# A hybrid attention and HGRN layer: gates in pieces, meta rows in 34 columns, and casts and splits pinned in order

## The chip, the cores and the metric

The kernel runs on one core of a Trainium2 chip. The core has five engines with queues of their own: TensorE (PE) multiplies matrices, VectorE (DVE), ScalarE (ACT) and GpSimd (POOL) work on tiles, and SyncE (SP) issues transfers. An engine takes the instructions of its queue in order, and one that waits holds up all behind it. The metric is device time in microseconds (us), the median of several runs.

## The reference

The kernel computes one decoder layer in float32. 16 meta tokens are put ahead of 1024 tokens, which makes 1040 rows of 1024 columns. Cut to what matters:

```python
a = rmsnorm(h, ln_mix_pre)
dq, dk, dv, hq, hf, hi, hg = split(a @ w_in)            # 1024 -> 7 x 512
y_diff = diff_attention(dq, dk, dv, ...)                # 4 heads, blocks of 128 rows, 2 maps each
y_hgrn = hgrn2(hq, hf, hi, hg, lb, gnorm)               # 4 heads, chunks of 16 rows
h = h + rmsnorm(concat(y_diff, y_hgrn) @ w_out, ln_mix_post)
u = conv1d(rmsnorm(h, ln_ffn_pre) @ w_up)               # 1024 -> 5632, 3 taps per channel
gate, up = split(u)
h = h + rmsnorm((gelu(gate) * up) @ w_down, ln_ffn_post)
return h[:, 16:]                                        # without the meta rows
```

## The kernel before

Every large product is made of three matmuls. An operand `x` is split into a high part, which ACT casts to the format that TensorE reads, and a low part, which POOL or DVE gets by subtracting the high part from `x`; the products high·high, high·low and low·high are added up in PSUM. For weights these are `wh` (high) and `wl` (low), made from the raw tile `wr` that a DMA has brought. `load_split` does this for one tile of 128 x 512, and `load_m` for the two tiles of a projection. The normalised input of the layer is kept in the same way, as `ahi` and `alo`, 8 slices of 128 rows by 1040 tokens.

The program runs in stages.

- *Heads.* For each of four heads the three projections of the attention (`dq`, `dk`, `dv`) and the four of the HGRN part (`hf`, `hq`, `hi`, `hg`) are made, in this order. Each goes over three groups of tokens (16+256, 384 and 384), 24 matmuls to a group, into a PSUM tile `pi_<name>_<group>`; `ev_q`, `ev_k`, `ev_v` and others take it out to SBUF (for `hg`: three ACT operations and one of DVE that make a sigmoid, `sg`). While PE makes the projections of the attention part, the HGRN part of the head before runs between the matmuls (tiles `pl`, `pd`, `mix`, `po`); while it makes those of the HGRN part, the attention blocks do (`S` scores, `pt` transposes, `at`, `pa` the weighted sum). `dense` is the generator of the projections; it takes the weights of the first projection itself and loads one projection ahead; `flush` sends out work that has been put off. `interleave` mixes the generators by the costs that they yield, and so sets PE's order.
- *Differences of the down weights.* `down_sums` loads four tiles of `w_down` at a time, subtracts them in pairs on DVE and stores the results, in pieces between the groups of projections.
- *Output projection.* `out_part` makes the product of the mixed rows with `w_out`, 8 slices k, in two halves of 512 columns. Block 0, the 16 meta rows, has only two rows that are worked out here; `out_meta` makes them with `out_part`: three matmuls for each k, with two columns of `m0` as the stationary side.
- *Up projection.* Tiles `ft` of channels, each with a gate side (`ug`) and an up side (`uu`), and each in two halves of the tokens, p=0 and 1. Sums of weights and of inputs replace one of the eight products (7 products in a `unit`, in PSUM tiles `pa`, `pb`, `pc`; partial results `x`, `u`). A unit ends with the convolution: ACT makes the first tap (`conv`'s activation), DVE adds the two others (`SCALAR_TENSOR_TENSOR` on a tile `c`), ACT applies gelu, POOL multiplies the two sides. `prep` makes the splits of the weights for the next `ft`.
- *Down projection*, in the same way, and the end of the layer.

What sets the order: on PE the instructions stand as the program writes them. On the other queues a scheduler of the framework orders them, by data and its own estimate, unless `issue_after` (`tc.issue_after(x)`, and `behind(...)` built on it) puts an instruction behind another one in its queue.

Of the kernel before, what the change touches and what calls it, by code (L numbers as in the profile page):

```python
# [17 lines left out]
P = 128  # L18
# [4 lines left out]
KD = D // P  # L23
# [22 lines left out]
class Ordered:  # L46
# [3 lines left out]
    def __getattr__(self, name):  # L50
        call = getattr(self.engine, name)

        def issue(*args, **kw):
            ins = call(*args, **kw)  # L54
            return self.tc.keep_in_program_order(ins) if self.state["ordered"] else ins

        return issue
# [29 lines left out]
def layer_kernel(ctx: ExitStack, tc: tile.TileContext, x, meta, table, lbl, gpre, gpost, win,  # L87
# [65 lines left out]

    def split(hi, lo, raw, eng=None):
        A.copy(hi, raw)
        (eng or G).tensor_tensor(lo, raw, hi.bitcast(F32), op=ALU.subtract)
# [23 lines left out]
    at_cm, atp = pool("at", 1)  # L180
    ahi = atp.tile([P, KD, L], F32R, tag="ahi", name="ahi")
    alo = atp.tile([P, KD, L], F32R, tag="alo", name="alo")
    ws_cm, wsp = pool("wdsums", 5)

    last_load = []
# [42 lines left out]
    def proj_step(pt, parts, k, t0, t1, evac):  # L228
        cost = max(115.0, 0.42 * (t1 - t0))
        hi, lo = parts[k // 4]  # L230
        s = slice(P * (k % 4), P * (k % 4 + 1))
        T.matmul(pt, hi[:, s], ahi[:, k, t0:t1], start=(k == 0), stop=False)
        yield cost
        T.matmul(pt, hi[:, s], alo[:, k, t0:t1], start=False, stop=False)
        yield cost
        T.matmul(pt, lo[:, s], ahi[:, k, t0:t1], start=False, stop=(k == KD - 1))
        if k == KD - 1:
            evac()
        yield cost
# [35 lines left out]
    def pre_hi(pv, ks, s):  # L275
        return A.copy(ahi[:, ks, s], pv)

    def pre_lo(pv, ks, s):
        return V.tensor_tensor(alo[:, ks, s], pv, ahi[:, ks, s].bitcast(F32), op=ALU.subtract)

# [303 lines left out]
    def attn_in(h):  # L584
# [8 lines left out]
        def ev_q(g, b0, b1, t0, t1, pt):  # L593
            for m in range(2):
                A.mul(qs[m][own[m], t0:t1], pt[own[m]], 0.125)
                V.scalar_tensor_tensor(qs[m][oth[m], t0:t1], pt[own[m]], 0.125, qs[m][own[m], t0:t1].bitcast(F32), ALU.mult, ALU.subtract)

        def ev_k(g, b0, b1, t0, t1, pt):
            for m in range(2):
                A.copy(ks[m][own[m], t0:t1], pt[own[m]])  # L600
                V.tensor_tensor(kl[m][own[m], t0:t1], pt[own[m]], ks[m][own[m], t0:t1].bitcast(F32), op=ALU.subtract)
                A.copy(ks[m][oth[m], t0:t1], pt[own[m]])

# [7 lines left out]
    def attn(h, tens):  # L611
# [128 lines left out]

    def dense(tiles, preload=None, side=iter(())):
        parts = preload
        for idx, (m, name, evac) in enumerate(tiles):
            if parts is None:
                parts = load_m(m, name)
            nxt = load_m(tiles[idx + 1][0], tiles[idx + 1][1]) if idx + 1 < len(tiles) else None
            for g in range(3):
                next(side, None)
                for step, c in enumerate(proj_group(g, parts, name, evac)):
                    if step == 8:  # L750
                        flush()
                    yield c
            parts = nxt
# [173 lines left out]

    def load_wo(n, k):
        raw = wp.tile([P, 512], F32, tag="wr", name=f"wor{n}_{k}", bufs=3)
# [7 lines left out]
        hi, lo = (where.tile([P, 512], F32R, tag=t, name=f"{t}{n}_{k}", bufs=bufs) for t in tag)  # L937
        split(hi, lo, raw, V if n or k else G)
        return hi, lo
# [4 lines left out]
    def mix_split(i, k0, k1):  # L944
        r, t0 = tok(i)
        src = mix(slice(k0, k1), t0, t0 + r)
        if i < 2:
            m = (m0, kept)[i]
            hi, lo = m[:, 0, k0:k1], m[:, 1, k0:k1]
        elif k1 - k0 == 1:  # L950
# [25 lines left out]

    def out_meta(py, wo, nk):
        return out_part((m0[:, 0], m0[:, 1], 0, nk, 2), py, wo, True, True)

# [33 lines left out]
    def out_first():  # L1013
# [5 lines left out]
        for j in range(2):  # L1019
# [3 lines left out]
            A.copy(y0[:, FIRST[j]], pys[j])  # L1023
        for n, i in enumerate(FIRST[2:]):
            for k in ((0, 1), (2, 3), (4,), (5,), (6,), (7,))[n]:
                wo.append(load_wo(1, k))
            if n == 3:
# [6 lines left out]
            yield from out_part(sq_, py, wo0, False, True)  # L1034
            A.copy(y0[:, i], py)
        py = ps_in("py0_0")
        yield from out_meta(py, wo0, 7)
        A.copy(y0[:2, 0], py[:2])
        while 0 not in finished:
# [176 lines left out]
    for n, i in enumerate(order):  # L1216
# [5 lines left out]
        if i < 2:  # L1222
            m = (m0, kept)[i]
            todo = [(m[:, 0, a:a + 2], m[:, 1, a:a + 2], a, a + 2, tok(i)[0]) for a in range(0, KD, 2)]
        else:
            todo = ms + [pre_last[i]]
        nxt = []
        for c, part in enumerate(todo):
# [8 lines left out]
            if c == 3 and n >= 2:  # L1237
                trans(order[n - 2])
            for _ in out_part(part, py, wo, c == 0, part is todo[-1]):
                pass  # L1240
# [13 lines left out]
        if i == 3:  # L1254
            prep_plain(1, ("12", "22"))
        post_a(i, py)
    post_b(8)
# [19 lines left out]

    def conv(ft, p, side, u):
# [4 lines left out]
        V.scalar_tensor_tensor(c, u[:, 1:1 + w], cwt[:, m, 1:2], c, ALU.mult, ALU.add)  # L1283
        V.scalar_tensor_tensor(c, u[:, 0:w], cwt[:, m, 0:1], c, ALU.mult, ALU.add)
        return c

    def gated(ft, p, ug, uu, cu=None):
        cg = conv(ft, p, 0, ug)
        A.activation(cg, cg, AF.Gelu_apprx_tanh)
        cu = cu or conv(ft, p, 1, uu)  # L1290
        G.tensor_tensor(cg, cg, cu, op=ALU.mult)  # L1291
        st = SY.dma_start(gsc[P * ft: P * (ft + 1), 2 * HALF * p:2 * HALF * (p + 1)], cg)
        if ft < 2 and p == 0:
            marks["store"] = st

    waiting = []

    def plain_unit(ft, p, bank):
# [17 lines left out]
        if ft and p:  # L1316
            waiting.extend(us)
        else:
# [4 lines left out]
    def unit(ft, p, bank):  # L1323
# [39 lines left out]
        seam(p, (ug, uu))  # L1363
        gated(ft, p, ug, uu)
        yield
# [56 lines left out]
    for ft in range(2, NF):  # L1422
        units = [unit(ft, p, ps_b) for p in range(2)]
        for j in range(7):
            if j > 3 or ft > 2:
                prep(7 * (ft + 1) + j)
            for p, u in enumerate(units):
                next(u)
                if (ft, j, p) == (2, 3, 0):
                    with behind("u3", "x1"):  # L1430
                        cu = conv(1, 1, 1, waiting[1])
            if (ft, j) == (2, 3):
                with behind("u3", "shift"):
                    for q in range(4):
                        prep(21 + q)
                    gated(1, 1, *waiting, cu)
        if ft == NF - 3:
# [285 lines left out]
```

## Time and profile before

| | |
|---|---|
| time, median of 3 runs | 1327.34 us (1326.83 to 1329.81) |
| profiled execution | 1325.77 us, its span 1324.0 us |
| TensorE busy | 1276.6 us, 96%, 10227 matmuls |
| VectorE busy | 912.8 us, 69% |
| ScalarE busy | 689.4 us, 52% |
| GpSimd busy | 413.5 us, 31% |
| mean granted clock of TensorE | 0.994 |

The span is the time from the first to the last instruction in one profiled execution. A busy share is an average over all stages. In the profile a row of the timeline gives the start in us, the duration in us, the engine, the line of the kernel, the operation, the tile written and the tiles read, and the shape; in brackets stands how long the engine was idle ahead of it and what released it. Buffer numbers are left out there (`wh_dq` is any tile of that name). Where a helper records the operation all rows have its line, L54. A row of grouped instructions gives least, median and most ns.

### The profile page before, as it was taken

How to read it: one execution, taken by the hardware profiler on the slowest of the kernel's cores; microseconds unless marked ns; L12 is line 12 of the kernel's file. 1: busy time of each engine (PE TensorE's matmuls, PEld its weight loads, DVE VectorE, ACT ScalarE, POOL GpSimd, SP SyncE). 2: the span in 40 equal slices, each digit the busy share in tenths (PEclk: the TensorE clock that was granted, in tenths of full speed). 3: DMA queues.
4: the chain of work that ended last, by engine and by line, in shares of the span. 5: the costliest groups of instructions: out<-in, count | busy, mean ns of one | idle time of the engine just before them, and what ended most of it. 6: DMA issues, size and time to landing. Idle time of an engine off the chain costs nothing.

```text
span 1324.0 us, 26317 instructions
## 1 busy us (share of the span) xinstructions
PE 1276.6 (96%) x10227; PEld 1181.8 (89%) x10227; DVE 912.8 (69%) x1589; ACT 689.4 (52%) x1670; POOL 413.5 (31%) x324
## 2 busy tenths in 40 slices
PE   6999999999999999999999799999999999999997
PEld 5898899989999999777899799999999998888886
DVE  7666557564756465834778777877787876697587
ACT  7465346535654565545665454554454454554454
POOL 3211211121202120112147567667667641010021
PEclk9999999999999999999999899999999999999999
DMA  6331323132311011835713222222222324964363
GB/s 217 109 127 61 101 94 132 56 129 77 124 44 35 33 33 46 262 114 182 242 41 112 84 84 76 92 80 82 81 89 76 105 85 166 343 222 156 107 207 120
DMA packets 84371, 153.07 MB, mean 116 GB/s; under 512 B 9571, under 2 KB 19843, under 8 KB 84246
## 3 DMA queue, kind: packets, MB, share of 16 engines
q1 hardware_dynamic: 84246, 151.39, 34.0%
q8 instruction: 80, 1.31, 0.4%
q14 instruction: 45, 0.37, 0.1%
HBM read 112.69 MB, written 38.67 MB: 114 GB/s over the span
## 4 chain that ended last, share of the span: by engine, by line
PE 71%; DVE 6%; DMA 3%; ACT 3%; issue 2%; POOL 1%; SPq 1%; DVEq 0%; ACTq 0%; POOLq 0%
PE pd L1534 5%; PE pd L1535 5%; PE pd L1533 5%; PE pb L1336 4%; PE pb L1337 4%; PE pb L1338 4%; PE pa L1337 2%; PE pa L1336 2%; PE pa L1338 2%; PE pa L709 2%; PE pc L1338 2%; PE pc L1337 2%; PE pc L1336 2%; PE py L970 2%; PE py L974 2%
## 5 line engine op out<-in xcount | busy, mean ns | idle before, releaser
L1336 PE MATMUL pb<-t,uh 128*128 128x258 f32 (+1 forms) x480 | 135.4, 282 | 10.7 <-DVE u L54 10.7
L1337 PE MATMUL pb<-t,uh 128*128 128x258 f32 (+1 forms) x480 | 135.1, 281 | 0.0
L1338 PE MATMUL pb<-t,ul 128*128 128x258 f32 (+1 forms) x480 | 134.9, 281 | 0.0
L1534 PE MATMUL pd<-wl,gh 128*128 128x512 f32 (+1 forms) x314 | 121.4, 386 | 0.5 <-DVE wl L54 0.5
L1535 PE MATMUL pd<-wh,gl 128*128 128x512 f32 (+1 forms) x314 | 120.6, 384 | 0.0
L1533 PE MATMUL pd<-wh,gh 128*128 128x512 f32 (+1 forms) x314 | 120.1, 383 | 0.0
L54 DVE SCALAR_TENSOR_TENSOR c<-uu,cwt,c 128x512 f32<-128x512 f32 x88 | 92.4, 1050 | 22.5 <-ACT c L54 21.9
L1291 POOL TENSOR_TENSOR c<-c,c 128x512 f32<-128x512 f32 x44 | 68.4, 1554 | 124.1 <-ACT c L54 118.1
L1336 PEld LDWEIGHTS pb<-t,uh 128*128 128x128 f32 x480 | 91.5, 191 | 11.3 <-DVE u L54 11.3
L1337 PEld LDWEIGHTS pb<-t,uh 128*128 128x128 f32 x480 | 91.6, 191 | 0.0
L1338 PEld LDWEIGHTS pb<-t,ul 128*128 128x128 f32 x480 | 91.4, 190 | 0.0
L1337 PE MATMUL pa<-t,uh 128*128 128x258 f32 (+1 forms) x320 | 89.8, 281 | 0.0
L1338 PE MATMUL pa<-t,ul 128*128 128x258 f32 (+1 forms) x320 | 89.7, 280 | 0.0
L1336 PE MATMUL pa<-t,uh 128*128 128x258 f32 (+1 forms) x320 | 89.7, 280 | 0.0
L54 DVE SCALAR_TENSOR_TENSOR c<-ug,cwt,c 128x512 f32<-128x512 f32 x88 | 87.6, 996 | 1.7 <-ACT c L54 1.1
L1338 PE MATMUL pc<-t,ul 128*128 128x256 f32 x320 | 88.3, 276 | 0.0
L1336 PE MATMUL pc<-t,uh 128*128 128x256 f32 x320 | 88.3, 276 | 0.0
L1337 PE MATMUL pc<-t,uh 128*128 128x256 f32 x320 | 88.3, 276 | 0.0
L1534 PEld LDWEIGHTS pd<-wl,gh 128*128 128x128 f32 x314 | 59.0, 188 | 13.6 <-DVE wl L54 1.6
L1533 PEld LDWEIGHTS pd<-wh,gh 128*128 128x128 f32 x314 | 58.9, 188 | 12.6
L1535 PEld LDWEIGHTS pd<-wh,gl 128*128 128x128 f32 x314 | 59.0, 188 | 11.5
L54 ACT ACTIVATE pb<-S,ast 128x528 f32<-128x528 f32 (+7 forms) x72 | 46.5, 647 | 39.1 <-DVE ast L54 38.9
(411 smaller groups left out, 4210.3 us busy)
## 6 DMA issues: line engine op xcount, KB each, us to landing
ra<-in_wup_dram SPq DMA_DIRECT2D x80, 256.0 KB, 2.7
wd<-in_wdown_dram SPq DMA_DIRECT2D x44, 256.0 KB, 4.2
tsc<-wd SPq DMA_DIRECT2D x44, 256.0 KB, 2.7
gsc<-c SPq DMA_DIRECT2D x44, 256.0 KB, 2.0
wi<-tsc SPq DMA_DIRECT2D x44, 256.0 KB, 2.8
gi<-gsc SPq DMA_DIRECT2D x33, 256.0 KB, 3.7
wi<-in_wdown_dram SPq DMA_DIRECT2D x33, 256.0 KB, 3.0
msc<-mm SPq DMA_DIRECT2D x21, 256.0 KB, 3.5
```

Of the source, the lines that this page charges most:

```text
L54: ins = call(*args, **kw)
L709: T.matmul(po[:, :P], w_, vn[:, j], start=(j == 0), stop=(j == i))
L970: T.matmul(py[:r], mh[:, j, :r], hi, start=(first and j == 0), stop=False)
L974: T.matmul(py[:r], ml[:, j, :r], hi, start=False, stop=(last and k == k1 - 1))
L1291: G.tensor_tensor(cg, cg, cu, op=ALU.mult)
L1336: T.matmul(pt, hi[:, s], th[:, k], start=(first and k == 0), stop=False, skip_group_check=True)
L1337: T.matmul(pt, hi[:, s], tl[:, k], start=False, stop=False, skip_group_check=True)
L1338: T.matmul(pt, lo[:, s], th[:, k], start=False, stop=(k == 3), skip_group_check=True)
L1533: T.matmul(py, gh[:, s], wh, start=(k == 0 and pr not in (3, 7)), stop=False, skip_group_check=True)
L1534: T.matmul(py, gh[:, s], wl, start=False, stop=False, skip_group_check=True)
L1535: T.matmul(py, gl[:, s], wh, start=False, stop=(k == NH - 1), skip_group_check=True)
```

## The change

1. *Gates in pieces.* The second half's convolution and gate of tiles 1, 2 and 3 is not made at the end of its unit. It is put on the list `waiting` and made within the next `ft`: the first taps on ACT at step 1, the other taps at step 3. `conv` becomes `shift` and `taps`, and `gate` is the product.
2. *Meta rows.* `m0` holds high and low parts in 36 columns: the high parts of the two rows in columns 0 and 1, the low ones in 32 and 33, zeros between. Two matmuls per k (with the high and with the low part of the weights) have 34 columns of `m0` as the stationary side; rows 0 and 1 of the result and rows 32 and 33 are then added with a copy on ACT and an addition on DVE.
3. *Activations by group.* `ahi` and `alo` become three tiles each, one for each group of tokens.
4. *Pinned order.* `in_turn(eng)` puts an instruction behind the last one that the program has issued on `eng` so far. `load_split` uses it for the cast on ACT. `down_sums` uses it for each difference, with one step more between tiles. `load_wo` for the second half holds back its splits and issues them ahead of the next block, behind ACT's and DVE's last.
5. *Order in the projections and blocks.* `ev_q` and `ev_k` issue their ACT operations ahead of the DVE ones. `dense` calls `flush` at step 14 of a group instead of 8. Around the last block of the attention the generator yields more cost.

```diff
+    def in_turn(eng):
+        return tc.issue_after(eng.last.ins)
+
-    def split(hi, lo, raw, eng=None):
-        A.copy(hi, raw)
-        (eng or G).tensor_tensor(lo, raw, hi.bitcast(F32), op=ALU.subtract)
+    def split(hi, lo, raw, eng=None, turn=()):
+        with ExitStack() as st:
+            for e in turn:
+                st.enter_context(in_turn(e))
+            A.copy(hi, raw)
+            (eng or G).tensor_tensor(lo, raw, hi.bitcast(F32), op=ALU.subtract)
...
-        split(hi, lo, raw)
+        split(hi, lo, raw, turn=(A,))
         return hi, lo
...
-                V.tensor_tensor(b[d], b[p_], b[q_], op=ALU.subtract)
+                with in_turn(V):
+                    V.tensor_tensor(b[d], b[p_], b[q_], op=ALU.subtract)
...
                 load(k + 1)
                 yield
+                yield
...
         def ev_k(g, b0, b1, t0, t1, pt):
             for m in range(2):
                 A.copy(ks[m][own[m], t0:t1], pt[own[m]])
+                A.copy(ks[m][oth[m], t0:t1], pt[own[m]])
+            for m in range(2):
                 V.tensor_tensor(kl[m][own[m], t0:t1], pt[own[m]], ks[m][own[m], t0:t1].bitcast(F32), op=ALU.subtract)
-                A.copy(ks[m][oth[m], t0:t1], pt[own[m]])
...
+            if i + 1 == NBLK:
+                yield 1
             yield from apply(i)
             if i + 2 < NBLK:
                 yield from ahead
             if i + 2 == NBLK:
-                yield 2
+                yield 3
...
-                    if step == 8:
+                    if step == 14:
                         flush()
...
-    m0 = yp.tile([P, 2, KD, 2], F32R, tag="m0", name="m0")
+    m0 = yp.tile([P, KD, 36], F32R, tag="m0", name="m0")
+    G.memset(m0.bitcast(F32), 0.0)
...
+            while held:
+                split(*held.pop(0), turn=(A, V))
             for k in ((0, 1), (2, 3), (4,), (5,), (6,), (7,))[n]:
-                wo.append(load_wo(1, k))
+                wo.append(load_wo(1, k, True))
...
-    def out_meta(py, wo, nk):
-        return out_part((m0[:, 0], m0[:, 1], 0, nk, 2), py, wo, True, True)
+    def out_meta(py, wo, k0, k1, last):
+        for k in range(k0, k1):
+            for l in range(2):
+                T.matmul(py[:34], m0[:, k, :34], wo[k][l], start=(k == 0 and l == 0), stop=(k == last and l == 1))
+                yield 216
...
+        A.copy(y0[:2, 0], py[32:34])
+        V.tensor_tensor(y0[:2, 0], y0[:2, 0], py[:2], op=ALU.add)
...
+        if p and ft < LATE:
+            waiting.append((ft, p, ug, uu))
+        else:
+            gated(ft, p, ug, uu)
...
+                if late and (j, p) == (3, 0):
+                    with behind("u3"):
+                        taps(f, 1, uu, cu)
+            if late and j == 1:
+                f, q, ug, uu = waiting[0]
+                with behind("u2", "x1"):
+                    cu, cg = shift(f, q, 1, uu), shift(f, q, 0, ug)
+                with behind("u2", "shift"):
+                    prep(7 * (ft + 1) + (ft > 2))
+            if late and j == 3:
+                with behind("u3", "shift"):
+                    taps(f, 0, ug, cg)
+                    A.activation(cg, cg, AF.Gelu_apprx_tanh)
+                    gate(f, q, cg, cu)
+                    for i in (3,) if ft > 2 else (1, 2, 3):
+                        prep(7 * (ft + 1) + i)
+                waiting.pop(0)
```

In the following rows of the queues a name ends with its group or block and the number of its buffer; `x2` is two in a row.

ACT before, at the end of head 1's HGRN projections and the start of head 2's `dq` (the last `dq` cast stood 17 rows ahead of these):

```order
L54 ACTIVATE sg_1_3137<-pi_hg_1_3076 128x384
L54 ACTIVATE sg_1_3137<-sg_1_3137,one 128x384
L54 ACTIVATE sg_1_3137<-sg_1_3137 128x384
L54 CAST wh_dk_0_3196<-wr_dk_0_3195 128x512
L54 CAST wh_dk_1_3202<-wr_dk_1_3201 128x512
L54 ACTIVATE sg_2_3170<-pi_hg_2_3145 128x384
L54 ACTIVATE sg_2_3170<-sg_2_3170,one 128x384
L54 ACTIVATE sg_2_3170<-sg_2_3170 128x384
L54 ACTIVATE q_2_3176<-pi_dq_0_3209 64x272
```

ACT after, at the same place:

```order
L54 ACTIVATE sg_2_3159<-pi_hg_2_3117 128x384
L54 ACTIVATE sg_2_3159<-sg_2_3159,one 128x384
L54 ACTIVATE sg_2_3159<-sg_2_3159 128x384
L54 CAST wh_dq_0_3173<-wr_dq_0_3172 128x512
L54 CAST wh_dq_1_3179<-wr_dq_1_3178 128x512
L54 CAST wh_dk_0_3185<-wr_dk_0_3184 128x512
L54 CAST wh_dk_1_3191<-wr_dk_1_3190 128x512
L54 ACTIVATE q_2_3165<-pi_dq_0_3198 64x272
```

All four casts now stand behind the last `sg`, and ahead of the first `q`.

ACT before, during head 1's `dk` projection, where the casts of `hf` were, well ahead of `dv`:

```order
L54 CAST k_1_1587<-pi_dk_1_1977 64x384
L54 CAST wh_hf_0_2321<-wr_hf_0_2320 128x512
L54 CAST k_1_1587<-pi_dk_1_1977 64x384
L54 CAST k_1_1588<-pi_dk_1_1977 64x384 x2
L54 CAST wh_hf_1_2327<-wr_hf_1_2326 128x512
L54 CAST k_1_1587<-pi_dk_2_2075 64x384
L54 COPY kn_0_2130<-pk_0_2131 128x384
```

ACT after, at the end of head 1's `dv`, where they are now:

```order
L54 ACTIVATE nss_2_2299<-nss_2_2299,eps 128x3
L54 ACTIVATE nss_2_2299<-nss_2_2299 128x3
L54 COPY vt_2_2314<-pi_dv_2_2237 128x384
L54 CAST wh_hf_0_2321<-wr_hf_0_2320 128x512
L54 CAST wh_hf_1_2327<-wr_hf_1_2326 128x512
L54 CAST wh_hq_0_2333<-wr_hq_0_2332 128x512
L54 COPY avn_1586<-pn_va_2_2377 128x384
```

They moved behind the copy of the last `dv` group.

DVE before, between tiles `ft` 2 and 3 of the up projection, up to the first partial result of tile 3 (`u_3_0`; `c_2_1` is the second half of tile 2):

```order
L54 SCALAR_TENSOR_TENSOR c_2_0_8623<-uu_0_8379,cwt,c_2_0_8623 128x512
L54 SCALAR_TENSOR_TENSOR c_2_1_8649<-uu_1_8398,cwt,c_2_1_8649 128x512
L54 SCALAR_TENSOR_TENSOR c_2_0_8618<-ug_0_8378,cwt,c_2_0_8618 128x512
L54 SCALAR_TENSOR_TENSOR c_2_0_8623<-uu_0_8379,cwt,c_2_0_8623 128x512
L54 SCALAR_TENSOR_TENSOR c_2_0_8618<-ug_0_8378,cwt,c_2_0_8618 128x512
L54 TENSOR_TENSOR ug_1_8397<-pc_1_8457,u_2_1_8400 128x256
L54 SCALAR_TENSOR_TENSOR c_2_1_8649<-uu_1_8398,cwt,c_2_1_8649 128x512
L54 TENSOR_TENSOR ul_8656<-ra_11_8657,uh_8655 128x512
L54 SCALAR_TENSOR_TENSOR c_2_1_8644<-ug_1_8397,cwt,c_2_1_8644 128x512
L54 TENSOR_TENSOR ul_8708<-ws_8709,uh_8707 128x512
L54 SCALAR_TENSOR_TENSOR c_2_1_8644<-ug_1_8397,cwt,c_2_1_8644 128x512
L54 TENSOR_TENSOR u_3_0_8672<-pb_0_8713,x_3_0_8671 128x256
```

DVE after, at the same place:

```order
L54 SCALAR_TENSOR_TENSOR c_2_0_8619<-uu_0_8375,cwt,c_2_0_8619 128x512 x2
L54 TENSOR_TENSOR ug_0_8374<-pc_0_8458,u_2_0_8377 128x256
L54 TENSOR_TENSOR ug_1_8393<-pc_1_8471,u_2_1_8396 128x256
L54 SCALAR_TENSOR_TENSOR c_2_0_8614<-ug_0_8374,cwt,c_2_0_8614 128x512
L54 TENSOR_TENSOR ul_8641<-ra_11_8642,uh_8640 128x512
L54 SCALAR_TENSOR_TENSOR c_2_0_8614<-ug_0_8374,cwt,c_2_0_8614 128x512
L54 TENSOR_TENSOR u_3_0_8657<-pb_0_8692,x_3_0_8656 128x256
L54 TENSOR_TENSOR u_3_1_8676<-pb_1_8706,x_3_1_8675 128x256
L54 TENSOR_TENSOR ul_8725<-ws_8726,uh_8724 128x512
L54 TENSOR_TENSOR u_3_0_8658<-pb_0_8692,x_3_0_8656 128x256
L54 SCALAR_TENSOR_TENSOR c_2_1_8720<-uu_1_8394,cwt,c_2_1_8720 128x512
```

The four operations on `c_2_1` and one `ul<-ws` moved behind `u_3_0`.

More of the change, by code (lines that the diff above doesn't have):

```diff
@@ L180, in layer_kernel, with act @@
     at_cm, atp = pool("at", 1)
-    ahi = atp.tile([P, KD, L], F32R, tag="ahi", name="ahi")
-    alo = atp.tile([P, KD, L], F32R, tag="alo", name="alo")
+    line_up(atp, 32)
+    acts = [[atp.tile([P, KD, start(b1 - 1) + P - start(b0)], F32R, tag=f"a{l}{g}", name=f"a{l}{g}") for g, (b0, b1) in enumerate(GROUPS)]
+            for l in ("hi", "lo")]
+    def act(l, ks, t0, t1):
+        g = 0 if t1 <= start(3) else 1 if t1 <= start(6) else 2
+        base = start(GROUPS[g][0])
+        return acts[l][g][:, ks, t0 - base:t1 - base]
     ws_cm, wsp = pool("wdsums", 5)
+    wsp.tile([P, 32], F32, tag="lineup_ws", name="lineup_ws", bufs=1)
     last_load = []
@@ L937, in load_wo @@
         hi, lo = (where.tile([P, 512], F32R, tag=t, name=f"{t}{n}_{k}", bufs=bufs) for t in tag)
-        split(hi, lo, raw, V if n or k else G)
+        if hold:
+            held.append((hi, lo, raw, V))
+        else:
+            split(hi, lo, raw, V if n or k else G)
         return hi, lo
@@ L1035, in out_first @@
             A.copy(y0[:, i], py)
+        while held:
+            split(*held.pop(0), turn=(A, V))
         py = ps_in("py0_0")
-        yield from out_meta(py, wo0, 7)
-        A.copy(y0[:2, 0], py[:2])
+        yield from out_meta(py, wo0, 0, 7, 6)
+        A.copy(y0[:2, 0], py[32:34])
+        V.tensor_tensor(y0[:2, 0], y0[:2, 0], py[:2], op=ALU.add)
         while 0 not in finished:
@@ L1222, in layer_kernel @@
         if i < 2:
[L1223 to L1224 removed]
+            todo = [(kept[:, 0, a:a + 2], kept[:, 1, a:a + 2], a, a + 2, P) for a in range(0, KD, 2)]
         else:
@@ L1238, in layer_kernel @@
                 trans(order[n - 2])
-            for _ in out_part(part, py, wo, c == 0, part is todo[-1]):
+            for _ in out_part(part, py, wo, c == 0, part is todo[-1]) if i else out_meta(py, wo, 2 * c, 2 * c + 2, KD - 1):
                 pass
@@ L1255, in layer_kernel @@
             prep_plain(1, ("12", "22"))
+        if i == 0:
+            low = qp.tile([P, 512], F32, tag="tmp", name="low", bufs=1)
+            A.copy(low[:2], py[32:34])
+            V.tensor_tensor(py[:2], py[:2], low[:2], op=ALU.add)
         post_a(i, py)
@@ L1424, in layer_kernel @@
         for j in range(7):
-            if j > 3 or ft > 2:
+            late = bool(waiting)
+            if not late or j > 3 or (ft > 2 and j in (0, 2)):
                 prep(7 * (ft + 1) + j)
```

50 lines of the change are left out of this document (26 added, 24 removed).

## The prediction

> **What bounds the kernel now.** I read the page's busy times first, then the waits of TensorE, and then the timeline at every place where the change moves something that TensorE waits for. The page:
>
> ```profile
> span 1324.0 us, 26317 instructions
> PE 1276.6 (96%) x10227; PEld 1181.8 (89%) x10227; DVE 912.8 (69%) x1589; ACT 689.4 (52%) x1670; POOL 413.5 (31%) x324
> ```
>
> TensorE (PE) is busy 1276.6 of 1324.0 us. So 47 us of idle time and the matmuls themselves are all that a change can take; other engines matter only where PE waits for them. The waits of PE, by who ended them (total us, times, longest):
>
> ```profile
> PE pb L1336 <- DVE u L54: 10.7, 3, 8.2
> PE pl L451 <- DVE mix L54: 5.6, 5, 2.5
> PE pt L685 <- DVE at L54: 2.3, 4, 1.0
> PE pa L709 <- ACT pb L54: 1.9, 3, 0.8
> PE pa L709 <- DVE at L54: 1.7, 3, 1.3
> PE pi_dv L232 <- DVE q L54: 1.7, 1, 1.7
> PE pi_dv L232 <- ACT k L54: 1.5, 3, 0.5
> PE pn_vh L347 <- ACT mix L54: 1.0, 3, 0.3
> PE pn_vh L347 <- ACT pb L54: 0.9, 1, 0.9
> PE pi_hf L232 <- ACT k L54: 0.8, 1, 0.8
> ```
>
> Two things stand out: one wait of 8.2 us in the up projection, and many waits of at most 2.5 us in the attention and HGRN stages.
>
> The sum below is made against the profiled execution, 1325.77 us (its span of 1324.0 and 1.77 around it). The median of the runs shown is 1327.34, 1.57 above, and the forecast is that median plus the sum. A change within 0.2% (2.7 us) is about what a measurement of this kernel can't tell from none.
>
> **1. Weight splits pinned on ACT: the cost.** In the changed order ACT casts `wh_dq_0` only after the three gate activations of `pi_hg_2`, and `wh_hf_0` only after `vt_2<-pi_dv_2`. PE goes from the last matmul of `pi_hg_2` straight to `pi_dq_0`, and from `pi_dv_2` straight to `pi_hf_0`. Before, these casts stood well ahead, and PE crossed without a gap. The first switch to dq, and the durations of each link:
>
> ```profile
> 142.87 0.34 PE L236 MATMUL pi_hg<-ahi,wl_hg 128*128 128x384 f32 x1
> 143.29 0.29 PE L236 MATMUL pi_dq<-ahi,wl_dq 128*128 128x272 f32 x1
> 143.64 0.48 ACT L54 ACTIVATE sg<-pi_hg 128x384 f32<-128x384 f32 x1
> 145.34 0.62 ACT L54 ACTIVATE sg<-sg,one 128x384 f32<-128x384 f32 x1 [1.22 <-DVE sg L54]
> 145.99 0.53 ACT L54 ACTIVATE sg<-sg 128x384 f32<-128x384 f32 x1
> L54 DVE TENSOR_SCALAR sg<-sg x12: 301/356/1152, 132.3 to 531.0; 128x384 f32<-128x384 f32 x8, 128x272 f32<-128x272 f32 x4
> L54 ACT CAST wh_dq<-wr_dq x8: 618/620/645, 8.9 to 384.3; 128x512 fp32r<-128x512 f32 x8
> L156 POOL TENSOR_TENSOR wl_hf<-wr_hf,wh_hf x8: 1263/1280/1292, 52.0 to 435.1; 128x512 fp32r<-128x512 f32 x8
> ```
>
> The last `pi_hg` matmul ends at 142.87+0.34=143.21. Then in series: ACT 0.48, DVE 0.36 (the median; the row's 1152 ns is with POOL at work beside it, and POOL now waits for the cast), ACT 0.62 and 0.53, cast 0.62, with some 0.04 of handing over at each of six steps. So the first `pi_dq` matmul starts near 146.05. The third needs the low half from POOL, 1.28 more, so it starts near 147.35 instead of 143.29: 4.06 us. This happens at three switches (heads 1, 2, 3), 12.2 us. What comes behind waits for nothing else: the second weight tile's cast and subtraction run while PE works through the 12 matmuls of the first. The switch to hf is shorter:
>
> ```profile
> 196.53 0.34 PE L236 MATMUL pi_dv<-ahi,wl_dv 128*128 128x384 f32 x1
> 196.96 0.29 PE L236 MATMUL pi_hf<-ahi,wl_hf 128*128 128x272 f32 x1
> 197.36 0.47 ACT L54 COPY vt<-pi_dv 128x384 f32<-128x384 f32 x1
> ```
>
> From 196.87: copy 0.47, cast 0.62, POOL 1.28, handing over 0.1, so 199.34 instead of 196.96: 2.4 each for heads 1 to 3. At head 0 PE waited 0.8 already (the `pi_hf` row above), which leaves 1.6. Together 8.8. **Term: +21.0.** Bounds: 19 with no handing over, 24 if POOL's subtraction shares time with DVE at four of the seven.
>
> **2. Gates in pieces: the gain.** The wait of 8.2 us and what follows it (times and durations; in the table the stretches with busy time and count of each engine, then the granted clock):
>
> ```profile
> 728.96 0.28 PE L1338 MATMUL pc<-t,ul 128*128 128x256 f32 x1
> 737.44 0.58 PE L1336 MATMUL pb<-t,uh 128*128 128x256 f32 x1 [8.20 <-DVE u L54]
> 727.51 0.92 DVE L54 SCALAR_TENSOR_TENSOR c<-uu,cwt,c 128x512 f32<-128x512 f32 x1 [2.03 <-ACT c L54]
> 731.71 0.74 DVE L54 SCALAR_TENSOR_TENSOR c<-uu,cwt,c 128x512 f32<-128x512 f32 x1
> 732.37 0.68 DVE L54 TENSOR_TENSOR ul<-ra,uh 128x512 fp32r<-128x512 f32 x1
> 732.97 1.75 DVE L54 SCALAR_TENSOR_TENSOR c<-ug,cwt,c 128x512 f32<-128x512 f32 x1
> 734.64 1.74 DVE L54 TENSOR_TENSOR ul<-ws,uh 128x512 fp32r<-128x512 f32 x1
> 736.31 0.74 DVE L54 SCALAR_TENSOR_TENSOR c<-ug,cwt,c 128x512 f32<-128x512 f32 x1
> 736.97 0.74 DVE L54 TENSOR_TENSOR u<-pb,x 128x256 f32<-128x256 f32 x2
> 737.40:742.50 5.10, 5.06 (x24) 5.07 (x25) 2.53 (x4) 1.02 (x3) 4.55 (x4) 0.51 0.28 99
> 742.50:747.00 4.50, 4.50 (x40) 4.50 (x40) 1.54 (x3) 1.89 (x4) 2.24 (x2) 1.00 0.16 58
> ```
>
> DVE reaches `u_3_0` at 736.97 only. Ahead of it stand the four gate operations of tile 2's second half (`c_2_1`, at 727.51, 731.71, 732.97 and 736.31; the order in the section on the change tells which they are) and `ul<-ws`, and the change puts all five behind it. That takes away the 2.03 of waiting, 0.92, 0.74, 1.75, 1.74 and 0.74: 7.9 us of the way to 736.97. `u_3_0` then stands near 729.05. PE went on 0.47 behind it and could have gone on at 737.44−8.20=729.24, so 0.3 of the wait is left; I take 0.6, since the cast for `ul<-ra` may hold DVE a little. Of 8.2 that is 7.6. The 24 matmuls behind the wait took 5.10 us at a granted clock of 0.51, and 40 then took 4.50 at 1.00, so 24 would take 2.70: 2.4 more that go with the wait. The same four operations now fall between the `u` and `uu` of the next tile. DVE's work there is four additions of 0.37 and four gate operations of 0.74 to 1.75, so 4.4 to 8.5 us, against three groups of 24 matmuls, 8.1 us, that PE does meanwhile. I cost it at nothing; without that cover it is 0.4 at each of tiles 3 and 4, and with a wait for ACT like the 2.03 above up to 2.4 at each. **Term: −10.0**, bounds −10.6 and −5.
>
> **3. Meta rows in 34 columns.** The rows of the 16 kept-apart tokens' product, 11 steps apart:
>
> ```profile
> 605.46 0.39 PE L970 MATMUL py<-woh,m 128*2 128x512 f32 x1
> 608.00 0.39 PE L974 MATMUL py<-woh,m 128*2 128x512 f32 x1
> ```
>
> 2.54/11 = 0.231 us from start to start, whatever the stationary side holds. Three products per k become two: 7 fewer in the first half of the columns and 8 in the second, 15 × 0.231. The added copy and addition on two rows lie beside the following blocks' matmuls; if they were on the path they would be under 1 us twice. **Term: −3.5.**
>
> **4. Order of the projections' evacuations, the later flush, the extra steps, the pinned differences.** Both ACT halves of q and k now come ahead of the DVE halves, so `pi_dv <- ACT k` (1.5) goes, and the prologue's `pi_dv <- DVE q` (1.7), since two other DVE operations no longer stand between its two halves. The differences of the down weights, which wait for a DMA on DVE, are issued one at a time between fixed neighbours, so they no longer bunch ahead of a `mix` or `at` that PE wants. PE does two or three other groups before the last block's `pt` and `pa`, and arrives 4 us later after each switch of part 1 while DVE works its backlog off. I take from the rows: k 1.5, q 1.7, both `pn_vh` 1.9, 3.7 of the 5.9 of `pt` and `pa` (the last blocks), and 4.1 of the 5.6 of `pl <- mix`: the two longest, which lie 12 and 20 us behind the switches at 143 and 273:
>
> ```profile
> 155.37 0.51 PE L451 MATMUL pl<-mix,kr 128*32 128x16 f32 x40 [1.59 <-DVE mix L54]
> 272.69 0.34 PE L236 MATMUL pi_hg<-ahi,wl_hg 128*128 128x384 f32 x1
> 293.07 0.83 PE L451 MATMUL pl<-mix,kr 128*32 128x16 f32 x64 [2.48 <-DVE mix L54]
> ```
>
> That is the whole of what I expect to go. What is late next is the rest of those rows, and stays. **Term: −12.9.** Bounds: −3.2 (only what the rearranged q and k touch) and −18.
>
> **5. Activations by group, line-up tiles, moved DMAs.** The matmuls read the same columns; loads of weights land well before the new, later casts. The output projection's held splits follow DVE instead of preceding, on engines with free time. POOL's memset of `m0` is off the path. Cost nothing; up to 1 us if a held weight is late, since `py` stands behind it.
>
> **Sum:** 21.0 − 10.0 − 3.5 − 12.9 = −5.4. Against the profiled execution that gives 1320.4; on the median, 1327.34 − 5.4 = 1321.9, so **1322**.
>
> **The rivals.**
> *The cover is not bought back (slower).* The pins of part 1 cost their 21 us, but DVE's backlog in the blocks is not what the moved steps relieve, and PE meets the same waits later: part 4 shrinks to its lower bound, −3.2, which adds 9.7, 1331.6. A part 4 of 7.5 leaves the time as it was, and below 4.8 it is slower by over 0.2%. For it: the nine rows other than the first share 17.4 us among many owners, and the added order also holds DVE back for a late DMA. Against: a 4 us pause just before these waits lets DVE catch up.
>
> *The long wait stays.* `u_3_0` depends on `x` and on the previous products as well, and if ACT's casts hold `ul<-ra` (0.68, still ahead of it) DVE gains little: 10 us less, 1332. Against: 7.9 us of DVE's rows ahead of it are plainly gone.
>
> *The clock falls at the dq switch.* There PE idles 2.8 us, does two matmuls and idles some 1.1 more. After the idle of 8.20 the clock was 0.51 for 24 matmuls, which cost 2.4; three times that is 7.2, 1329. Against it is the stall of 2.48 ahead of 293.07:
>
> ```profile
> 293.00:298.00 5.00, 4.52 (x148) 4.09 (x148) 4.84 (x15) 1.00 (x3) 0.00 (x0) 1.00 0.13 46
> ```
>
> The 5 us behind it have a clock of 1.00, so the threshold lies between 2.48 and 8.20, and 2.8 with a break is nearer the first. The Trainium skill ("TensorE: Matmul & The Clock Gate", Part 1: The HAM clock gate) says that the default clock is the slow half, and that an idle window of some 3.4 us brings it back; its table of advice says to keep idle gaps under about 3 us. The trace agrees with the half (0.51). By that rule alone the 2.8 us stay just short, and the sum would be unchanged; two idle pieces that the monitor counted together would exceed it.
>
> *All the stage waits go.* The pauses let DVE clear everything: part 4 reaches −18 and the rest of the prologue's waits go too, 1315.
>
> **How the numbers follow.** The forecast holds 0.42, with 1316 to 1328 as its own range from the bounds of parts 1, 2 and 4. The cover not bought back 0.18, the long wait staying 0.10, the clock 0.12, all waits gone 0.18. Faster by over 0.2% (below 1324.7) is 0.34 of the forecast and all of the last, 0.52. Within 0.2% is 0.08 of the forecast, 0.08 of the clock and 0.06 of the two slower ones, 0.22. Slower is the remaining 0.26. The range of 1313 to 1333 leaves out under 2 in 10.
>
> **What would show it.** The trace after should have gaps of some 2.8+1.1 us ahead of `pi_dq` at three places, and 1.2+1.2 ahead of `pi_hf` at four; no wait over 2 us in the up projection and no stretch at half clock there; 30 matmuls on `m0` instead of 45, all with 34 columns; and under 6 us in the rows `pl`, `pt`, `pa`, `pn_vh` that sum to 13.4 now. The forecast is wrong if the gaps at the switches are shorter (the order on ACT is not what I read) or if those rows keep their sum.

## The result, and the profile after

The changed kernel takes 1344.49 us (1343.13 to 1346.05) against 1327.09 us for the kernel before on the same chip. The ratio is 1.0142, with a 95% interval of 1.0121 to 1.0163: slower by 17.4 us, where 1322 was forecast and the range ended at 1333. The profiled execution has a span of 1342.8 us against 1324.0, so the two traces differ by 18.8 us.

The page of the changed kernel, with the busy time of each engine:

```profile
span 1342.8 us, 26290 instructions
PE 1284.9 (96%) x10212; PEld 1191.8 (89%) x10212; DVE 922.5 (69%) x1591; ACT 687.6 (51%) x1671; POOL 411.6 (31%) x325
```

TensorE executes 15 matmuls fewer and is busy 8.3 us longer. Its share of busy time is 96% as before, which says nothing: the matmuls themselves became longer somewhere. Those of its waits on which the account rests, in the same columns as before (total us, times, longest):

```profile
PE pb L1382 <- DVE u L54: 9.1, 3, 4.1
PE pi_dq L249 <- ACT wh_dq L54: 8.1, 3, 2.7
PE pi_hf L249 <- ACT wh_hf L54: 4.4, 4, 1.1
PE pi_hf L253 <- POOL wl_hf L163: 3.4, 4, 0.9
PE pa L728 <- DVE at L54: 2.7, 3, 1.2
PE pi_dq L253 <- POOL wl_dq L163: 2.6, 3, 1.0
PE pn_vh L364 <- ACT pb L54: 1.9, 3, 1.3
PE pt L704 <- DVE at L54: 1.8, 3, 1.0
PE py L996 <- ACT woh L54: 1.8, 1, 1.8
PE pl L468 <- DVE mix L54: 1.3, 3, 0.6
PE pa L728 <- ACT pb L54: 0.6, 2, 0.3
```

The four new rows of `pi_dq` and `pi_hf` are the switches; they sum to 18.5 us. The row of the up projection fell from 10.7 to 9.1 only. Where the stages begin is read from the first start in the rows of a tile (the first `py` is the end of the heads, the first `pq` that of the output projection, the first `pd` that of the up projection). Before:

```profile
L970 PE MATMUL py<-wh,mm x14: 391/396/504, 529.3 to 569.5; 128*128 128x512 f32 x14
L1310 PE MATMUL pq<-t,uh x128: 276/281/365, 654.4 to 700.8; 128*128 128x256 f32 x96, 128*128 128x258 f32 x32
L1533 PE MATMUL pd<-wh,gh x314: 276/388/398, 1104.5 to 1316.5; 128*128 128x512 f32 x147, 128*128 128x256 f32 x10
```

After:

```profile
L996 PE MATMUL py<-wh,mm x14: 388/394/497, 551.3 to 592.2; 128*128 128x512 f32 x14
L1356 PE MATMUL pq<-t,uh x128: 275/281/366, 674.1 to 720.5; 128*128 128x256 f32 x96, 128*128 128x258 f32 x32
L1592 PE MATMUL pd<-wh,gh x314: 279/394/398, 1123.2 to 1335.4; 128*128 128x512 f32 x147, 128*128 128x256 f32 x10
```

| stage | before | after | difference |
|---|---|---|---|
| heads | 529.3 | 551.3 | +22.0 |
| output projection | 125.1 | 122.8 | −2.3 |
| up projection | 450.1 | 449.1 | −1.0 |
| down projection, to the last start | 212.0 | 212.2 | +0.2 |

So all the loss is in the stage of the heads. The switches are what the prediction said in kind, and their waits are a little shorter. Timeline of TensorE at one switch to `dq` and one to `hf`, with the wait in brackets:

```profile
417.01 0.40 PE L249 MATMUL pi_dq<-ahi,wh_dq 128*128 128x272 f32 x1 [2.68 <-ACT wh_dq L54]
418.36 0.40 PE L253 MATMUL pi_dq<-ahi,wl_dq 128*128 128x272 f32 x1 [0.83 <-POOL wl_dq L163]
198.91 0.39 PE L249 MATMUL pi_hf<-ahi,wh_hf 128*128 128x272 f32 x1 [1.08 <-ACT wh_hf L54]
200.29 0.39 PE L253 MATMUL pi_hf<-ahi,wl_hf 128*128 128x272 f32 x1 [0.87 <-POOL wl_hf L163]
```

What the waits don't explain is the clock. At each of the six switches of heads 1 to 3 a stretch at half clock begins. The stretches, with their length and the busy time and count of each engine; the third number from the end is the granted clock:

```profile
143.12:149.94 6.82, 6.07 (x87) 5.48 (x87) 1.91 (x3) 1.32 (x3) 4.75 (x4) 0.50 0.67 176
201.14:204.56 3.42, 3.42 (x18) 3.42 (x17) 0.36 (x2) 0.10 (x1) 1.58 (x2) 0.50 0.82 248
279.64:286.48 6.84, 5.65 (x83) 5.04 (x84) 1.81 (x3) 1.81 (x4) 5.29 (x4) 0.50 0.42 146
337.68:341.08 3.40, 3.40 (x18) 3.40 (x17) 0.37 (x2) 0.00 (x0) 1.76 (x2) 0.50 0.91 246
419.60:423.00 3.40, 3.40 (x78) 3.12 (x77) 1.76 (x2) 0.62 (x1) 2.45 (x2) 0.50 0.91 286
474.20:477.62 3.42, 3.42 (x17) 3.42 (x17) 0.36 (x2) 0.00 (x0) 1.64 (x2) 0.50 0.81 237
```

Four are 3.4 us long and two are 6.8. At half clock TensorE does half of what it would, so a stretch of 3.4 us in which it is busy throughout costs 1.7. In the two long ones it idles for 0.75 and 1.19 us of the switch itself. Busy time times what the clock lacks comes to 12.7 us over the six. So the heads' 22.0 are the switches' 18.5, the clock's 12.7, and −9.2 of waits that went and of small change.

### The profile page after: what moved, and what is told of

Read it like the earlier page. It is cut to its first block, busy times and chain, and to the rows that moved or that the text cites. A ratio compares the mean times of both kernels' runs of the same rounds, so it can differ in the third digit from the quotient of the medians.

```text
span 1342.8 us, 26290 instructions
## 1 busy us (share of the span) xinstructions
PE 1284.9 (96%) x10212; PEld 1191.8 (89%) x10212; DVE 922.5 (69%) x1591; ACT 687.6 (51%) x1671; POOL 411.6 (31%) x325
## 4 chain that ended last, share of the span: by engine, by line
PE 64%; issue 17%; DVE 9%; ACT 5%; POOL 2%; DMA 2%; SPq 0%; DVEq 0%; POOLq 0%; ACTq 0%
PE pd L1593 5%; PE pd L1594 5%; PE pd L1592 5%; PE pb L1382 4%; PE pb L1383 4%; PE pb L1384 4%; PE pa L1383 2%; PE pa L1382 2%; PE pa L1384 2%; PE pc L1383 2%; PE pc L1382 2%; PE pc L1384 2%; DVE c L54 2%; PE pa L728 1%; PE py L996 1%
## 5 line engine op out<-in xcount | busy, mean ns | idle before, releaser
L54 DVE SCALAR_TENSOR_TENSOR c<-uu,cwt,c 128x512 f32<-128x512 f32 x88 | 98.3, 1117 | 19.8 <-ACT c L54 19.2
L1592 PEld LDWEIGHTS pd<-wh,gh 128*128 128x128 f32 x314 | 59.1, 188 | 11.5
L1204 POOL TENSOR_TENSOR ws<-ra,ra 128x512 f32<-128x512 f32 x40 | 59.0, 1474 | 14.2 <-DMA ra<-in_wup_dram 9.5
```

What stands on the lines that cost most here:

```text
L1204: G.tensor_tensor(sums[nm], a, b, op=op)
L1592: T.matmul(py, gh[:, s], wh, start=(k == 0 and pr not in (3, 7)), stop=False, skip_group_check=True)
```

## The experiments

Three questions: are the pinned weight casts the whole loss; how much of it is waiting and how much the clock; and where the gains of the other parts went. The comparison is with the kernel before on the same chip, some 1328 us each time.

**The pins.** The first kernel is the changed one with one argument taken away.

```diff
-        split(hi, lo, raw, turn=(A,))
+        split(hi, lo, raw)
```

> The changed kernel, with the weight casts of load_split not pinned behind ACT's last instruction any more; all else as changed. Theory P (the pins cost waits at the seven switches, 18.5 us in the trace after, and some 10 us of half clock behind them): 1344.5 - 18.5 - 10 = 1316, up to 1324 if waits of the attention blocks that the pauses had swallowed come back. Rival R (the other moved steps cost the time, the switches only collect it): the waits appear at other places and it stays above 1335.

Measured 1317.1 us, ratio 0.9925 (0.9905 to 0.9946). No wait for `wh_dq` or `wh_hf` is left, and the heads end at 523.1:

```profile
L996 PE MATMUL py<-wh,mm x14: 388/393/499, 523.1 to 565.0; 128*128 128x512 f32 x14
```

The pins cost 27.4 us in the changed kernel. Without them it beats both kernels. The reverse, the kernel before with the pin alone (the same line added, and what `turn` needs):

> The kernel before, with nothing changed but load_split's cast pinned behind ACT's last instruction. Theory P: 1327.1 + 17.7 (18.5 of waits, less 0.8 that was there) + 10 of half clock = 1355, down to 1347 if the pauses swallow waits of the blocks. Rival R: at most 1340. For the clock: at half speed for some microseconds behind each dq switch, as in the changed kernel.

Measured 1354.25 us, ratio 1.0206 (1.0188 to 1.0225), 26 us above the kernel before. The rows of the switches are those of the changed kernel:

```profile
PE pi_dq L236 <- ACT wh_dq L54: 8.1, 3, 2.7
PE pl L455 <- DVE mix L54: 5.7, 6, 1.7
PE pi_hf L236 <- ACT wh_hf L54: 4.4, 4, 1.1
```

The row `pl` waits 5.7 us as it does without the pin (5.6). So a pause of 4 us just before does not clear the backlog of DVE that this row shows, though part 4 had argued that it would.

**The place, or the pin?** The next kernel keeps every pin, but the program issues the first weights of the next part ahead of the second group of the last projection.

```diff
             for g in range(3):
                 next(side, None)
+                if g == 1 and nxt is None and then:
+                    soon.append(load_m(*then))
...
```

> The changed kernel with its pins kept, but the program issues the first weights of the next part of heads (dq of heads 1 to 3, hf of heads 1 to 3) one projection group after the first group of the last projection, so that the pin puts the casts behind an earlier ACT operation. Theory P (the place in the queue costs, not the pin): the waits at six of the seven switches go with the clock behind them, 1344.5 - 16.5 - 12.7 = 1315, up to 1320 with waits that come back; head 0's switch to hf keeps 2.0. If a pinned cast is costly wherever it stands: over 1330.

Measured 1317.56 us, ratio 0.9918 (0.9895 to 0.9940), the same as without pins. So the cost comes from where in the program the cast is issued, since the pin turns that place into the place in the queue. Of the seven switches one is left, head 0's.

**The clock, apart from the waits.** Matmuls of no use fill the idle time, so that the weights come as late as in the changed kernel and only the clock differs. They write the PSUM tile that the group then starts anew; `fill` is 28 ahead of the first group of a `dq` and 16 ahead of that of an `hf`.

```diff
         pt = ps_in(f"pi_{name}_{g}")
+        for _ in range(fill):
+            T.matmul(pt[:, :n], act(0, 0, 0, P), act(0, 1, t0, t1), start=True, stop=True)
...
```

> The changed kernel with its pins, and matmuls of no use (28 ahead of the first pi_dq group of heads 1 to 3, 16 ahead of the first pi_hf group of each head; they write the PSUM tile that the group then starts anew) in the place of the idle time at the switches. The weights come as late as before, so the waits' length stays lost; only the clock differs. Theory C (of the loss some 12.7 us, six windows at half clock, come from the clock monitor and not from the waits): 1344.5 - 12.7 = 1332, and a granted clock of 1.00 behind the switches. If the slow matmuls there have another cause: 1344.

Measured 1337.73 us, ratio 1.0074 (1.0050 to 1.0097): 6.8 us less than the changed kernel, half of what was expected. No stretch at half clock was left in the heads. The switches themselves are as long as in the changed kernel: in head 1, from the end of the projection before to the first product with low weights, 4.06 us instead of 4.04 at `dq` and 2.49 instead of 2.47 at `hf`. The rest is lost behind the switches to `hf`: from that product to the end of `hg` head 1 takes 77.3 us here and 75.4 in the next kernel. Why the longer fill does that is not shown. The next kernel fills only the first piece, 21 and 8 matmuls.

> The changed kernel with 21 idle matmuls ahead of pi_dq and 8 ahead of pi_hf, so that only the first, longer piece of each switch's idle time is filled and nothing is made longer. Theory C (six half-clock windows of 3.4 us cost 12.7 gross; 3 to 4 of it come back as waits that the slow stretches had hidden): no half-clock window in the stage of the heads, and 1344.5 - 9 = 1335. If the clock cost nothing net: 1344.

Measured 1332.27 us, ratio 1.0038 (1.0023 to 1.0053): 12.2 us less than the changed kernel, and more than was expected. Its switches take 4.04 and 2.47 us in head 1, as in the changed kernel. Its heads end at 541.0 instead of 551.3:

```profile
L1000 PE MATMUL py<-wh,mm x14: 388/393/499, 541.0 to 580.9; 128*128 128x512 f32 x14
```

So 10.3 of the 12.2 lie in the heads, where 2.4 of the clock's 12.7 come back as other time; the other 1.9 lie in later stages, where a stretch at half clock that the changed kernel has at 1078 (1.7 us) is missing. The granted clock over the heads of this kernel:

```profile
60.00:200.00 140.00, 135.06 (x1308) 128.41 (x1307) 79.05 (x185) 68.48 (x202) 26.24 (x29) 1.00 0.27 86
200.00:340.00 140.00, 135.16 (x1311) 128.94 (x1311) 81.39 (x191) 71.12 (x212) 23.52 (x25) 1.00 0.28 93
340.00:540.00 200.00, 191.60 (x1702) 183.76 (x1701) 119.25 (x270) 107.29 (x319) 30.57 (x31) 1.00 0.20 65
```

and of the changed kernel over the same times:

```profile
60.00:200.00 140.00, 130.82 (x1254) 123.78 (x1253) 79.68 (x185) 68.39 (x202) 23.94 (x27) 0.98 0.25 84
200.00:340.00 140.00, 131.50 (x1251) 125.18 (x1251) 79.17 (x181) 66.63 (x197) 24.50 (x26) 0.96 0.25 83
340.00:540.00 200.00, 187.98 (x1649) 179.68 (x1649) 119.91 (x271) 105.58 (x315) 31.16 (x31) 0.98 0.22 73
```

In the heads the pins cost 28.2 us (551.3 against 523.1 without them). So 10.3 of these are the clock, and the other 17.9 (541.0 against 523.1) are the waits, less what the pauses hide.

**The gates in pieces**, alone on the kernel before (the functions `shift`, `taps`, `gate`, `gated`, the list and the loop over the tiles as in the change):

> The kernel before, with the gates in pieces (waiting list, LATE = 4) alone. Theory G (the deferred gate is a debt that DVE pays at tile 4, where its own eight operations and the four of tile 3 meet): a wait of 3 to 5 us at tile 4 or 5 takes the place of the 8.2, and the time is 1325 to 1327. The prediction's term: -10, 1317.

Measured 1325.54 us, ratio 0.9986 (0.9972 to 1.0000). Two waits stand in the place of the 8.2, at the start of tile 3 and two tiles on (2.14 and 2.75, each with 3.4 us at half clock behind it). Then, on the unpinned kernel, the deferring alone was varied: `LATE = 2` and `LATE = 21` instead of 4.

> The unpinned kernel with LATE = 2: only tile 1's gate is put off, as in the kernel before. Theory G: the wait at tile 3 is back to some 8 us with two to three half-clock windows, and the one behind tile 4 gone: 1317 to 1320. The prediction's term (the gates in pieces are worth 10): 1327.

> The unpinned kernel with LATE = 21 instead of 4: the second half's gate of every tile is made within the next. Theory G (the debt is paid where the deferring ends, at tile 4): the wait of 2.7 at the tile behind it goes with its half-clock window of 1.7, that of 4.6 at tile 3 stays: 1317.1 - 4.4 = 1313. If tile 4 has nothing to do with it: 1317.

Measured 1316.61 (0.9915, 0.9898 to 0.9933) and 1316.38 (0.9913, 0.9893 to 0.9933), against 1317.1 for 4. The waits move much as expected; the time, for which 1313 was expected with 21, does not. Timeline rows at tile 3 for 4, 21 and 2:

```profile
726.87 0.46 PE L1382 MATMUL pb<-t,uh 128*128 128x256 f32 x1 [4.63 <-DVE u L54]
725.36 0.58 PE L1382 MATMUL pb<-t,uh 128*128 128x256 f32 x1 [3.66 <-DVE u L54]
728.65 0.58 PE L1382 MATMUL pb<-t,uh 128*128 128x256 f32 x1 [7.57 <-DVE u L54]
```

With 2 the long wait is back and the one of 2.7 behind tile 4 is gone; with 21 that one is gone too, but the wait at 1049 grew to 3.4 from 1.7, with 3.4 us at half clock behind it that were not there before. DVE's work is a debt that is paid at one place or another: in this comparison deferring the gates of tiles 2 and 3 gains nothing.

**Meta rows**, alone on the kernel before:

> The kernel before, with the meta rows in 34 columns alone. 15 matmuls fewer of 0.231 us: 1323.6. If 34 columns made each matmul slower than 2, or the copy and addition were on the path, 1325 to 1328.

Measured 1325.29 us, ratio 0.9986 (0.9973 to 1.0000), 1.9 us less with an interval that holds both 3.6 and 0. In the trace the output projection took 122.3 us (528.8 to 651.1) instead of 125.1, 2.8 less. The matmuls are no slower with 34 columns: eleven steps take 2.54 us (602.29 to 604.83), as they did with two.

**What the rest of the change does in the heads.** Two kernels undo one half each in the unpinned one: the turn of the differences (with its extra step), and the order of evacuations, flush and steps.

```diff
-                with in_turn(V):
-                    V.tensor_tensor(b[d], b[p_], b[q_], op=ALU.subtract)
+                V.tensor_tensor(b[d], b[p_], b[q_], op=ALU.subtract)
...
                 load(k + 1)
-                yield
                 yield
```

> The unpinned kernel without the turn of the differences (no in_turn(V), no extra step). If the pinned differences carry the 6.2 us that the stage of the heads gained: 1317.1 + 5 = 1322, with the waits of pl for mix back at 5 us. If the order in the projections and blocks carries it: 1317 to 1318.

Measured 1323.65 us, ratio 0.9970 (0.9956 to 0.9984), 6.5 us above the unpinned kernel; in its trace the heads end at 534.6, 11.5 later, of which the next two stages make up 3.9. The wait for `mix` is back (2.1 in the unpinned kernel), and one of its pieces, 1.95 us, has 3.4 us at half clock behind it:

```profile
PE pl L466 <- DVE mix L54: 5.0, 4, 2.0
```

> The unpinned kernel with the order of ev_q and ev_k, the flush at step 8 and the costs around the last block as in the kernel before; differences pinned. If these carry the 6.2 us of the heads: 1322 to 1323, with the wait of pi_dv for k and the prologue's for q back. If the differences carry it: 1317 to 1318.

Measured 1317.68 us, ratio 0.9931 (0.9915 to 0.9947). The time is that of the unpinned kernel, but not in the same place. The heads end 4.3 us later (527.4), with the wait of `pi_dv` for `k` at 5.4 us in three pieces, two of which have 3.4 us at half clock behind them. The output projection makes up for it: 119.6 us against 124.3. In the unpinned kernel its weights come late:

```profile
PE pi_dv L249 <- ACT k L54: 5.4, 3, 1.8
PE py L996 <- ACT woh L54: 2.2, 1, 2.2
```

The first row is of the kernel with the old order, the second of the unpinned one; behind the second stand 3.4 us at half clock, which cost 1.6 more. So the new order of the evacuations does what it should in the heads, and here loses it again to a weight that lands too late. The tiles of activations by group and the held splits of `w_out` were not taken out alone.

## Why the prediction was wrong, step by step

*Part 1, the pins: right.* Reckoned as the prediction did it, up to the first product with low weights, the three switches to `dq` take 4.04, 4.49 and 4.04 us and those to `hf` 2.44 to 2.48. Less what was there before (under 0.1 each, and 1.17 at head 0's `hf`) that is 20.8 us, where 21.0 was forecast. The path (sigmoid, cast, low half from POOL) is the one that was read from the order. The rows of the waits sum to only 18.5, since the two matmuls between the two waits take some 0.5 us by themselves and 0.25 in the stream. By the kernels with the fill and without the pins, 17.9 of it reaches the time.

*The clock: this is the step that failed.* The sum has no term for the clock. The prediction took it that the length of a wait decides, that the threshold "lies between 2.48 and 8.20" and that 2.8 is nearer the first; it priced a fall at three switches, 7.2 us, with a chance of 0.12. The runs showed falls at six switches, 12.7 us by the trace and 10.3 by the kernel with the fill. At the switches to `hf` two waits of 1.08 and 0.87 us were enough in three of four cases, while the single wait of 2.48 before was not. What counts is how much of one stretch of a fixed grid is idle (last section). The wait of 2.48 lay across a line of that grid, at 291.88, with 1.29 us on one side and 1.19 on the other. So one stall without consequence was taken for a threshold. The price of one fall was right in size: 2.4 was forecast, and the two long ones cost 3.0 and 2.8, the four short ones 1.7 each.

*Part 2, gates in pieces: this failed too, −10.0 forecast.* The stage became 1.0 us shorter, and 2.3 with the gates alone (450.1 to 447.8). There was to be no wait over 2 us in it and no stretch at half clock; there are two waits (3.21 and 4.14) and two stretches (at 795 and 1078). `u_3_0` was to stand 0.3 us behind what PE could use. In the changed kernel PE waited 3.21 there. DVE's rows ahead of it:

```profile
743.29 3.06 DVE L54 SCALAR_TENSOR_TENSOR c<-uu,cwt,c 128x512 f32<-128x512 f32 x2 [0.56 <-ACT c L54]
747.62 1.69 DVE L54 SCALAR_TENSOR_TENSOR c<-ug,cwt,c 128x512 f32<-128x512 f32 x1 [0.61 <-ACT c L54]
749.24 1.74 DVE L54 TENSOR_TENSOR ul<-ra,uh 128x512 fp32r<-128x512 f32 x1
750.90 0.74 DVE L54 SCALAR_TENSOR_TENSOR c<-ug,cwt,c 128x512 f32<-128x512 f32 x1
751.57 0.41 DVE L54 TENSOR_TENSOR u<-pb,x 128x256 f32<-128x256 f32 x1
```

Before, the slow 1.75 and 1.74 were among the operations that moved, and the prediction took them away with those. But slow rows stand in this place again: `ul<-ra` was 0.68 and became 1.74. In both traces the slow rows lie beside operations of POOL (from 732.20 to 735.84 before, from 747.46 to 750.43 here), and the operation of 0.74 behind them does not. But the `ul<-ra` of 0.68 before lies beside one too (732.37), and no run took POOL's work away, so that this cause is argued and not shown. Two waits of 0.6 for ACT come on top. And the "up to 2.4 at each" of tiles 3 and 4, costed at nothing, came as one wait of 4.14 us behind tile 4, where tile 3's four deferred operations meet tile 4's own eight:

```profile
795.57 0.58 PE L1382 MATMUL pb<-t,uh 128*128 128x256 f32 x1 [4.14 <-DVE u L54]
795.50:798.90 3.40, 3.33 (x17) 3.33 (x18) 1.55 (x4) 0.77 (x2) 3.32 (x3) 0.56 0.22 84
```

with 3.4 us near half clock behind it.

*Part 3, meta rows: −3.5 forecast.* −2.8 in its stage when alone; the interval of the time holds it. In the changed kernel the stage became 2.3 shorter, since `py` waits 1.8 us for `woh`, the late held weight that part 5 had put at nothing, or up to 1.

*Part 4: mis-sized, −12.9 forecast, −6.2 measured.* Without the pins the heads end at 523.1 instead of 529.3. The waits for `k` and `q` went as forecast (3.2), but the rows `pl`, `pt`, `pa` and `pn_vh`, which summed to 13.4 and were to keep under 6, keep 8.3 in the changed kernel, and a new wait of `pn_va` for `kn` adds 1.9. The reasons were half wrong as well. The pause behind a switch clears nothing (the row `pl` with the pin alone). What clears `pl` is the turn of the differences with its extra step, 6.5 us by the kernel without it, to which only 4.1 had been given.

*Together.* From −5.4: +10.3 for the clock, +9.0 for part 2, +6.7 for part 4, +1.2 for part 3, +0.2 in the down projection, −3.1 for part 1. That gives +18.9, against 18.8 in the traces and 17.4 in the times. Of the named slower cases the clock came true in full, the loss of part 2's gain nearly so and that of part 4's by two thirds; the range had been made for one at a time.

## What to carry to other kernels

A pin of the form "behind the last instruction that the program has issued" makes the place in the program the place in the queue. So look at what the program had issued last: here a load of weights stood at the start of a part, behind an evacuation that ended after TensorE could have started on these weights, and issuing it two projection groups earlier took away nearly all of the loss (1317.6 with the pins, 1317.1 without). When a change puts short idle times in front of a busy TensorE, add the clock: each 3.4 us at half clock cost 1.7 us here, and of the 28.2 us that the pins cost in the heads over a third was the clock. And look whether a long duration belongs to the instruction that shows it: here a row of 1.74 us stood in the same place of the queue after the instruction had moved.

## What the runs showed of the hardware

The granted clock fell for 3.4 us or a multiple of it (6.8 at two switches, 3.4 at four). The Trainium skill ("TensorE: Matmul & The Clock Gate", Part 1: The HAM clock gate) describes a monitor that watches a window of some 3.4 us, which runs freely and does not start anew with the kernel. The trace agrees. The eight falls of the changed kernel begin at 143.12 and 17, 40, 57, 81, 97, 191 and 274 times 3.413 us later, so they lie on one grid of 3.413 us. In each of the nine other traces with more than one fall they lie on such a grid too, each with its own start.

That explains why equal waits differ. In the kernel with the old order of evacuations the same wait came three times. Here are the first and the third, and the busy times in the stretch of the grid that the wait begins in and in the next one:

```profile
176.56 0.44 PE L249 MATMUL pi_dv<-ahi,wh_dv 128*128 128x384 f32 x1 [1.80 <-ACT k L54]
173.91:177.32 3.41, 1.61 (x13) 1.38 (x12) 1.06 (x3) 1.81 (x4) 0.00 (x0) 1.00 0.27 91
177.32:180.73 3.41, 3.41 (x15) 3.41 (x14) 0.99 (x3) 0.48 (x1) 0.00 (x0) 0.50 0.00 0
436.98 0.44 PE L249 MATMUL pi_dv<-ahi,wh_dv 128*128 128x384 f32 x1 [1.80 <-ACT k L54]
433.33:436.74 3.41, 1.84 (x15) 1.62 (x13) 2.05 (x4) 1.45 (x4) 0.12 (x1) 1.00 0.54 150
436.74:440.15 3.41, 3.17 (x23) 3.14 (x24) 0.99 (x3) 1.05 (x3) 0.00 (x0) 1.00 0.03 5
```

The first lay whole in one stretch, and the next stretch ran at half clock; the second of the three, at 306.66, went the same way. The third lay across the line at 436.74, and the clock stayed. The wait of 3.21 us in the changed kernel, 1.87 on one side of a line and 1.34 on the other, had no fall behind it either. Over all 13 traces (in three of them the grid is set by a single fall), from 30 us on and at full clock, 33 stretches were idle for 1.9 us or more, and each was followed by half clock; of the 77 with 0.9 to 1.6 us idle two were. In between both happened: of two waits that each lay whole in one stretch, 1.73 us at 1058.77 in the kernel before had no fall behind it, and 1.72 at 1076.99 in the changed one had. What decides there is open.

The advice of the Trainium skill (the same page, section "Why this matters for your kernels"), to avoid idle gaps of over some 3 us, is not enough here: 1.7 us, or 1.08 and 0.87 together, did it.
